# Every fourth weight group's low part made by an adding DMA

## The chip, the core and the metric

The kernel runs on one core of one Trainium2 chip. The metric is the device time of one execution in microseconds; lower is better. The core's engines are named as in the profile: PE multiplies matrices (PEld is its weight load), DVE is VectorE, ACT is ScalarE, POOL is GpSimd, and SP issues DMAs. 16 DMA engines serve the core.

## What is computed

One hybrid decoder layer on 256 tokens of width 2048: a gated FFN (width 5504) with a half residual, then a mixer whose input projection feeds a recurrent branch (RG-LRU) and a sparse attention branch (top 64 of the keys by an indexer), then a second FFN and a final norm.

```python
def reference(x, ...):
    x = x + 0.5 * swiglu(rms_norm(x, ffn1_norm), ffn1_w_gate, ffn1_w_up, ffn1_w_down)
    x = x + hybrid_mixer(rms_norm(x, mix_norm), w_in, ...)
    x = x + 0.5 * swiglu(rms_norm(x, ffn2_norm), ffn2_w_gate, ffn2_w_up, ffn2_w_down)
    return rms_norm(x, final_norm)

def swiglu(x, w_gate, w_up, w_down):
    return (silu(x @ w_gate) * (x @ w_up)) @ w_down

def hybrid_mixer(h, w_in, ...):
    rx, rgate, q, k, v, iq, ik, iw, g_rnn, g_attn = split(h @ w_in)
    y_rnn = rg_lru(conv(rx)) * gelu(rgate)
    y_attn = dsa_attention(q, k, v, iq, ik, iw, rel_bias)
    merged = sigmoid(g_rnn) * (y_rnn @ w_proj_rnn) + sigmoid(g_attn) * (y_attn @ w_proj_attn)
    return merged @ w_out
```

## The kernel before

All activations lie transposed, features on the 128 partitions and the 256 tokens along the row. Every matrix product is made in float32r with a split: a float32 value is a high part (rounded to float32r) and a low part (the value minus the high part). The activations are held as high and low side by side, 512 columns. For each 128x128 block of weights PE makes two matmuls: the high weights against all 512 columns (L111), and the low weights against the 256 high columns (L112).

The weights are read once, in order of use. A **group** is eight blocks, 128x1024 float32 or 512 KB, and is one row block of the array in HBM. `Stream` is the reader of one matrix. `load` (L79 and on) lets SP issue the DMA of one group into a tile `raw` from a pool of three. `pop` (L89 and on) hands out one block's pair; when the last group is used up it takes the next `raw` and makes two new tiles, `whi` and `wlo`, each from a pool of three, with `split` (L65 and on): ScalarE copies `raw` to `whi` (L68), and DVE subtracts `whi` from `raw` into `wlo` (L69). A tile of a pool is written anew when the tile of three groups earlier has been read for the last time, by PE for `whi` and `wlo`, by ScalarE and DVE for `raw`.

The products run in this order: FFN 1 (for each of 43 output blocks of the hidden width two groups of the gate matrix, then two of the up matrix; then for each of 16 output blocks 43 blocks of the down matrix, which is 5.4 groups); the small indexer columns; the streams iq, k, v, q, rx and rg (two groups an output block); the gate columns and the attention projection in turn (ga, pa), the same for the recurrent branch (gr, pr); out; FFN 2 as FFN 1. 806 groups pass through `wsp`, two of them by a path of its own for the indexer's columns.

Every engine works its instructions strictly in the order of its own queue. A scheduler at build time fixes that order, so an engine's row stands not quite where the Python line stands, but groups stay in order. After each product ScalarE copies one half of PSUM to SBUF (`tb`, L133), DVE adds the halves (`tt`, L135), and what follows belongs to the stage. GpSimd adds the squares for the norms (L178, L180), adds the attention biases to the mask (L507, L508) and issues a few loads, of which the 16 `xo` (L657), 128 KB each, are the largest. TensorE's clock is granted at one of two levels, 1.2 or 2.4 GHz; the profile gives it as a share of the higher one.

Of the kernel before, what the change touches and what calls it, by code (L numbers as in the profile page):

```python
# [11 lines left out]
F32 = mybir.dt.float32  # L12
F32R = mybir.dt.float32r
AF = mybir.ActivationFunctionType
ALU = mybir.AluOpType
# [3 lines left out]
P = 128  # L19
# [16 lines left out]
G = 8  # L36
# [7 lines left out]
def hybrid_layer(ctx: ExitStack, tc: tile.TileContext, a, out):  # L44
    nc = tc.nc
    V, A, T, GP = nc.vector, nc.scalar, nc.tensor, nc.gpsimd
# [18 lines left out]
    def split(hi, lo, src, scale=None):  # L65

        if scale is None:
            A.activation(hi, src, AF.Copy)  # L68
            V.tensor_tensor(lo, src, hi.bitcast(F32), op=ALU.subtract)  # L69
        else:  # L70
            A.activation(hi, src, AF.Copy, scale=scale)
            V.scalar_tensor_tensor(lo, src, scale, hi.bitcast(F32), op0=ALU.mult, op1=ALU.subtract)  # L72

    class Stream:


        def __init__(self, src):
            self.src, self.ahead, self.left, self.at = src, [], [], 0

        def load(self, parts=1):  # L80
            raw = wraw.tile([P, G * P], F32, name="raw")
# [7 lines left out]
        def pop(self):  # L89
            if not self.left:  # L90
                if not self.ahead:
                    self.load()
                raw = self.ahead.pop(0)
                hi = wsp.tile([P, G * P], F32R, name="whi")
                lo = wsp.tile([P, G * P], F32R, name="wlo")
                n, self.parts = G * P // self.parts, 1
                for i in range(0, G * P, n):
                    split(hi[:, i:i + n], lo[:, i:i + n], raw[:, i:i + n])
                self.left = [(hi[:, i * P:(i + 1) * P], lo[:, i * P:(i + 1) * P]) for i in range(G)]
            return self.left.pop(0)  # L100

# [287 lines left out]
    for k0 in range(0, KT, G):  # L389
        raw = wraw.tile([P, G * P], F32, name="raw")  # L390
        nc.sync.dma_start(raw[:, :G * 80], a["w_ikw"][:, k0 * 80:(k0 + G) * 80])
        hi = wsp.tile([P, G * P], F32R, name="whi")
        lo = wsp.tile([P, G * P], F32R, name="wlo")
# [365 lines left out]
```

## Time and profile before

| | |
|---|---|
| runs | 2343.24 and 2334.46 us, median 2338.85 |
| profiled execution | 2343.12 us, of which the span from the first to the last instruction is 2341.3 |
| PE busy | 2316.1 us, 99% |
| DVE busy | 1505.7 us, 64% |
| ACT busy | 1156.6 us, 49% |
| POOL busy | 95.0 us, 4% |
| weights and other bytes moved | 437.46 MB, 187 GB/s over the span |

A busy PE includes matmuls that overlap, so the share says that PE had work all the time, not that it ran at its peak. The rows below are of that one execution, with times in microseconds from the start of the span unless they are marked ns.

### The profile page before, as it was taken

What the parts mean: (1) busy time and instruction counts of PE and PEld (TensorE: products, weight loads), DVE (VectorE), ACT (ScalarE), POOL (GpSimd) and SP (SyncE); (2) the same over time, 40 slices, a digit from 0 to 9 for tenths busy, and PEclk for the clock granted to TensorE, in tenths of its full rate; (3) what the DMA queues carried; (4) which work ended last, traced back from release to release, by engine and by line L of the source; (5) the groups of instructions that cost most, each with busy time, mean ns of one, the idle gap of its engine ahead of it and who ended that gap; (6) DMA issues with size and microseconds to landing.
All of it is one profiled execution on the core that took longest, in us unless ns stands there. A gap on an engine that the chain in (4) does not pass through costs nothing.

```text
span 2341.3 us, 34677 instructions
## 1 busy us (share of the span) xinstructions
PE 2316.1 (99%) x13507; PEld 2024.9 (86%) x13507; DVE 1505.7 (64%) x2238; ACT 1156.6 (49%) x1689; POOL 95.0 (4%) x137
## 2 busy tenths in 40 slices
PE   8999999999999999999999999999999999999998
PEld 6888888888888888998888888888888888888887
DVE  6766666655555687778855566676666666664444
ACT  6444444444444455677644444455544444444443
POOL 0000000000000011001000000021000000000000
PEclk9999999999999999999999999999999999999999
DMA  6555555556565544454565655666665665566664
GB/s 219 184 190 192 190 189 189 189 192 199 199 199 193 201 162 144 152 182 161 175 191 186 188 185 186 193 209 200 189 189 189 189 190 190 189 191 192 191 189 144
DMA packets 128548, 437.46 MB, mean 187 GB/s; under 512 B 14416, under 2 KB 22976, under 8 KB 128384
## 3 DMA queue, kind: packets, MB, share of 16 engines
q1 hardware_dynamic: 127296, 432.84, 56.7%
q8 instruction: 105, 1.72, 0.3%
q0 software_dynamic: 912, 2.33, 0.3%
q14 instruction: 59, 0.48, 0.1%
q10 hardware_dynamic: 176, 0.09, 0.0%
HBM read 430.92 MB, written 4.22 MB: 186 GB/s over the span
## 4 chain that ended last, share of the span: by engine, by line
PE 94%; DVE 3%; DMA 1%; ACT 1%; issue 1%; SPq 0%; POOL 0%; DVEq 0%; ACTq 0%
PE mm L111 58%; PE mm L112 29%; PE mm L126 2%; PE mm L125 2%; PE mm L127 2%; DVE wlo L69 1%; DMA raw<-in_w_rg 1%; ACT whi L68 0%; DMA raw<-in_wu 0%; PE aux L435 0%; PE aux L575 0%; PE aux L576 0%; DVE hst L622 0%; PE aux L505 0%; DMA raw<-in_wg 0%
## 5 line engine op out<-in xcount | busy, mean ns | idle before, releaser
L69 DVE TENSOR_TENSOR wlo<-raw,whi 128x1024 fp32r<-128x1024 f32 (+2 forms) x807 | 987.0, 1223 | 729.8 <-ACT whi L68 727.4
L68 ACT ACTIVATE whi<-raw 128x1024 fp32r<-128x1024 f32 (+2 forms) x807 | 853.6, 1058 | 1116.9 <-PE mm L111 560.0
L111 PE MATMUL mm<-x1hl,whi 128*128 128x512 f32 x1376 | 482.5, 397 | 8.1 <-DVE x1hl L72 7.4
L111 PE MATMUL mm<-x3hl,whi 128*128 128x512 f32 x1376 | 477.3, 394 | 0.0
L111 PE MATMUL mm<-h,whi 128*128 128x512 f32 x1333 | 462.2, 394 | 0.0
L111 PE MATMUL mm<-x2hl,whi 128*128 128x512 f32 x1280 | 457.1, 400 | 0.0
L112 PE MATMUL mm<-x1hl,wlo 128*128 128x256 f32 x1376 | 384.2, 279 | 1.8 <-DVE wlo L69 1.8
L112 PE MATMUL mm<-x3hl,wlo 128*128 128x256 f32 x1376 | 381.8, 278 | 0.0
L112 PE MATMUL mm<-h,wlo 128*128 128x256 f32 x1333 | 369.7, 277 | 0.0
L112 PE MATMUL mm<-x2hl,wlo 128*128 128x256 f32 x1280 | 360.1, 281 | 3.6 <-DVE wlo L69 3.3
L111 PEld LDWEIGHTS mm<-x1hl,whi 128*128 128x128 f32 x1376 | 260.3, 189 | 69.8 <-ACT whi L68 7.6
L111 PEld LDWEIGHTS mm<-x3hl,whi 128*128 128x128 f32 x1376 | 258.5, 188 | 59.2
L111 PEld LDWEIGHTS mm<-h,whi 128*128 128x128 f32 x1333 | 250.5, 188 | 57.6
L111 PEld LDWEIGHTS mm<-x2hl,whi 128*128 128x128 f32 x1280 | 240.8, 188 | 57.5 <-issue 0.7
L112 PEld LDWEIGHTS mm<-x1hl,wlo 128*128 128x128 f32 x1376 | 260.2, 189 | 3.2 <-DVE wlo L69 3.1
L112 PEld LDWEIGHTS mm<-x3hl,wlo 128*128 128x128 f32 x1376 | 258.4, 188 | 0.0
L112 PEld LDWEIGHTS mm<-h,wlo 128*128 128x128 f32 x1333 | 250.2, 188 | 0.0
L112 PEld LDWEIGHTS mm<-x2hl,wlo 128*128 128x128 f32 x1280 | 241.8, 189 | 6.7 <-DVE wlo L69 5.8
L135 DVE TENSOR_TENSOR tt<-mm,tb 128x256 f32<-128x256 f32 x285 | 118.8, 417 | 1.8 <-ACT tb L133 1.8
L133 ACT ACTIVATE tb<-mm 128x256 f32<-128x256 f32 x285 | 104.2, 366 | 2.0 <-DVE zero L151 2.0
L142 DVE TENSOR_TENSOR tz<-tt,rstd 128x256 f32<-128x256 f32 x224 | 94.8, 423 | 6.9
L111 PE MATMUL mm<-yat,whi 128*128 128x512 f32 x256 | 91.2, 399 | 0.0
(192 smaller groups left out, 1987.6 us busy)
## 6 DMA issues: line engine op xcount, KB each, us to landing
raw<-in_wu SPq DMA_DIRECT2D x172, 512.0 KB, 3.6
raw<-in_wd SPq DMA_DIRECT2D x172, 512.0 KB, 4.1
raw<-in_wg SPq DMA_DIRECT2D x171, 512.0 KB, 3.6
raw<-in_w_q SPq DMA_DIRECT2D x32, 512.0 KB, 3.4
raw<-in_w_rx SPq DMA_DIRECT2D x32, 512.0 KB, 3.4
raw<-in_w_rg SPq DMA_DIRECT2D x32, 512.0 KB, 3.5
raw<-in_w_ga SPq DMA_DIRECT2D x32, 512.0 KB, 3.6
raw<-in_w_pa SPq DMA_DIRECT2D x32, 512.0 KB, 3.6
```

Source lines behind the costliest of these rows:

```text
L68: A.activation(hi, src, AF.Copy)
L69: V.tensor_tensor(lo, src, hi.bitcast(F32), op=ALU.subtract)
L111: T.matmul(ps, hi, x, start=(k == 0), stop=False)
L112: T.matmul(ps[:, S:], lo, x[:, :S], start=False, stop=(k == kts - 1))
L125: T.matmul(ps[:, :S], hi, x[:, :S], start=(k == 0), stop=False)
L126: T.matmul(ps[:, :S], hi, x[:, S:], start=False, stop=False)
L127: T.matmul(ps[:, :S], lo, x[:, :S], start=False, stop=(k == kts - 1))
L133: A.activation(b[:M], ps[:M, S:], AF.Copy)
L135: V.tensor_tensor(t[:M], ps[:M, :S], b[:M], op=ALU.add)
L142: V.tensor_tensor(o, t, r, op=ALU.mult)
```

## The change

Each `Stream` counts its groups. Three of four are made as before. For every fourth, ScalarE writes the high part (L100 in the changed kernel) and then the negated high part into the low tile (L101), and GpSimd issues a DMA that reads the same group from HBM a second time and adds it to what lies in the low tile (L102). SP's load of the group into `raw` stays, since the high part is made from it. Lines after L105 stand seven lines further down in the changed kernel (L111 is L118, L112 is L119, L133 is L140).

```diff
         def __init__(self, src):
-            self.src, self.ahead, self.left, self.at = src, [], [], 0
+            self.src, self.ahead, self.left, self.at, self.popped = src, [], [], 0, 0
@@ def pop(self):
                 n, self.parts = G * P // self.parts, 1
-                for i in range(0, G * P, n):
-                    split(hi[:, i:i + n], lo[:, i:i + n], raw[:, i:i + n])
+                self.popped += 1
+                if self.popped % 4 == 0:
+
+                    A.activation(hi, raw, AF.Copy)
+                    A.activation(lo, hi.bitcast(F32), AF.Copy, scale=-1.0)
+                    GP.dma_start(lo, self.src[self.popped - 1], accum_op=ALU.add)
+                else:
+                    for i in range(0, G * P, n):
+                        split(hi[:, i:i + n], lo[:, i:i + n], raw[:, i:i + n])
```

Where it lies in the queues. The next two fences are ScalarE's queue in FFN 1 around the fourth output block's gate and up groups. `h` is the split of a hidden block, `sg` its silu, `tb` the copy out of PSUM; what stands in brackets is what the instruction waits for (PE, DVE, Activation for ScalarE itself, DMAHW for SP's and DMASW for GpSimd's DMAs). Before:

```order
L68 ACTIVATE whi_527<-raw_525 128x1024 [waits DMAHW6_49,PE_49,Activation_49]
L238 ACTIVATE sg_382<-tz_380 128x256 [waits DVE_49]
L133 ACTIVATE tb_384<-mm_303 128x256 [waits Activation_49]
L68 ACTIVATE whi_550<-raw_548 128x1024 [waits DMAHW7_49,PE_49,Activation_49]
L68 ACTIVATE h_115<-h_390 128x256 [waits DVE_49]
L133 ACTIVATE tb_484<-mm_394 128x256
L68 ACTIVATE whi_572<-raw_570 128x1024 [waits DMAHW0_49,PE_49,Activation_49]
L238 ACTIVATE sg_490<-tz_488 128x256 [waits DVE_49,Activation_49]
L133 ACTIVATE tb_492<-mm_439 128x256 [waits Activation_49]
L68 ACTIVATE whi_613<-raw_611 128x1024 [waits DMAHW1_49,PE_49,Activation_49]
L68 ACTIVATE h_115<-h_498 128x256 [waits DVE_49]
```

After:

```order
L140 ACTIVATE tb_386<-mm_304 128x256
L100 ACTIVATE whi_529<-raw_527 128x1024 [waits DMAHW6_49,PE_49,Activation_49]
L101 ACTIVATE wlo_530<-whi_529 128x1024 [waits DMASW5_49,PE_49,Activation_49]
L68 ACTIVATE h_115<-h_392 128x256 [waits DVE_49]
L140 ACTIVATE tb_486<-mm_396 128x256
L68 ACTIVATE whi_553<-raw_551 128x1024 [waits DMAHW7_49,PE_49]
L245 ACTIVATE sg_492<-tz_490 128x256 [waits DVE_49]
L140 ACTIVATE tb_494<-mm_441 128x256 [waits PE_49]
L100 ACTIVATE whi_575<-raw_573 128x1024 [waits DMAHW0_49,PE_49]
L68 ACTIVATE h_115<-h_500 128x256 [waits DVE_49]
L101 ACTIVATE wlo_576<-whi_575 128x1024 [waits DMASW4_49,PE_49,Activation_49]
```

The groups `whi_529` and `whi_575` (`whi_527` and `whi_572` before) are adding ones: behind each high part stands the negated copy into `wlo`, the second time with a split of `h` between the two. Between them lies one ordinary group, `whi_553`. The order of the others is kept.

GpSimd's queue from the loads of the start to the first sums of squares, before:

```order
L297 DMA ident_103<-in_ident 128x128
L299 DMA cw_105<-in_conv_w 128x64
L301 DMA CM_107<-in_causal 128x256
L303 DMA rb_109<-in_rel_bias 32x16
L178 COPY sqsum_4996<-sq_4994 128x256 [waits DVE_49,PE_49,Activation_49]
L180 ISA
L180 TENSOR_TENSOR sqsum_4996<-sqsum_4996,sq_5122 128x256 [waits Activation_49,Pool_49]
```

After, from the same load on:

```order
L310 DMA rb_109<-in_rel_bias 32x16
L102 DMA wlo_274<-in_wg1 128x1024 [waits DVE_49,PE_49,Activation_49]
L102 DMA wlo_330<-in_wu1 128x1024 [waits DVE_49,Activation_49]
L102 DMA wlo_530<-in_wg1 128x1024 [waits DMASW5_49,DVE_49,Activation_49]
L102 DMA wlo_576<-in_wu1 128x1024 [waits DMASW4_49,DVE_49,Activation_49]
L102 DMA wlo_787<-in_wg1 128x1024 [waits DMASW0_49,DMASW7_49,DVE_49,Activation_49]
L102 DMA wlo_833<-in_wu1 128x1024 [waits DMASW1_49,DVE_49,Activation_49]
```

The adding loads now stand where GpSimd had nothing to do: all of the gate and up matrices' come ahead of the first `sqsum`, in the order of the groups, each behind a wait for ScalarE's copy. In the down stage they alternate with the `sqsum` additions.

PE's queue at the start of such a group, before (an ordinary group at the same place):

```order
L112 MATMUL mm_502<-x1hl_111,wlo_506 128x256
L111 MATMUL mm_502<-x1hl_111,whi_527 128x512 [waits Activation_49]
L112 MATMUL mm_502<-x1hl_111,wlo_528 128x256 [waits DVE_49]
L111 MATMUL mm_502<-x1hl_111,whi_527 128x512
L112 MATMUL mm_502<-x1hl_111,wlo_528 128x256
```

After:

```order
L119 MATMUL mm_504<-x1hl_111,wlo_508 128x256
L118 MATMUL mm_504<-x1hl_111,whi_529 128x512 [waits Activation_49]
L119 MATMUL mm_504<-x1hl_111,wlo_530 128x256 [waits DMASW6_49]
L118 MATMUL mm_504<-x1hl_111,whi_529 128x512
L119 MATMUL mm_504<-x1hl_111,wlo_530 128x256
```

The order of the matmuls is the same. The first matmul with `wlo_530` waits for GpSimd's DMA, where the one with `wlo_528` waited for DVE, and it stands second in its group.

## Rows read from the trace of the kernel before

**Rows 1.** The page, busy us (share) xinstructions, and granted clock over 40 slices

```profile
PE 2316.1 (99%) x13507; PEld 2024.9 (86%) x13507; DVE 1505.7 (64%) x2238; ACT 1156.6 (49%) x1689; POOL 95.0 (4%) x137
...
PEclk9999999999999999999999999999999999999999
```

**Rows 2.** The page, chain of work that ended last, by engine and line

```profile
PE 94%; DVE 3%; DMA 1%; ACT 1%; issue 1%; SPq 0%; POOL 0%; DVEq 0%; ACTq 0%
PE mm L111 58%; PE mm L112 29%; PE mm L126 2%; PE mm L125 2%; PE mm L127 2%; DVE wlo L69 1%; DMA raw<-in_w_rg 1%; ACT whi L68 0%; DMA raw<-in_wu 0%; PE aux L435 0%; PE aux L575 0%; PE aux L576 0%; DVE hst L622 0%; PE aux L505 0%; DMA raw<-in_wg 0%
```

**Rows 3.** Waits: engine, line, waited for: us in total, times, longest us

```profile
PEld mm L112 <- DVE wlo L69: 8.9, 11, 1.4
...
PE mm L112 <- DVE wlo L69: 5.2, 7, 1.1
```

**Rows 4.** Timeline in FFN 1: start us, us, instruction [idle before, releaser]

```profile
401.38 1.06 ACT L68 ACTIVATE whi<-raw 128x1024 fp32r<-128x1024 f32 x1 [1.41 <-PE mm L111]
...
402.35 0.36 ACT L133 ACTIVATE tb<-mm 128x256 f32<-128x256 f32 x1
...
402.47 1.23 DVE L69 TENSOR_TENSOR wlo<-raw,whi 128x1024 fp32r<-128x1024 f32 x1 [1.21 <-ACT whi L68]
...
404.15 1.06 ACT L68 ACTIVATE whi<-raw 128x1024 fp32r<-128x1024 f32 x1 [1.44 <-PE mm L111]
```

**Rows 5.** The page, costliest groups: count, busy us, mean ns, idle before

```profile
L69 DVE TENSOR_TENSOR wlo<-raw,whi 128x1024 fp32r<-128x1024 f32 (+2 forms) x807 | 987.0, 1223 | 729.8 <-ACT whi L68 727.4
L68 ACT ACTIVATE whi<-raw 128x1024 fp32r<-128x1024 f32 (+2 forms) x807 | 853.6, 1058 | 1116.9 <-PE mm L111 560.0
```

**Rows 6.** SP's loads by stream: issue ns min/median/max, first to last start us

```profile
L84 SPq DMA_DIRECT2D raw<-in_w_q x32: 327/328/328, 824.2 to 933.5; - x32
L84 SPq DMA_DIRECT2D raw<-in_w_rx x32: 327/328/328, 936.0 to 1044.4; - x32
L84 SPq DMA_DIRECT2D raw<-in_w_rg x32: 327/328/332, 1048.1 to 1145.7; - x32
...
L84 SPq DMA_DIRECT2D raw<-in_w_iq x16: 327/328/542, 728.2 to 771.7; - x16
```

**Rows 7.** DMA: queue's packets, MB, share; loads' count, KB, us to landing

```profile
q1 hardware_dynamic: 127296, 432.84, 56.7%
...
raw<-in_wu SPq DMA_DIRECT2D x172, 512.0 KB, 3.6
...
xo<-x1d POOLq DMA_DIRECT2D x16, 128.0 KB, 3.4
...
wa<-in_rg_w_a SPq DMA_DIRECT2D x16, 64.0 KB, 2.6
...
DMA to landing us min/median/max: 2.4/3.4/5.1
```

**Rows 8.** Windows at the start: busy by engine, granted clock, DMA share, GB/s

```profile
12.00:16.00 4.00, 4.00 (x22) 3.19 (x20) 4.00 (x9) 3.97 (x9) 0.00 (x0) 1.00 1.02 400
```

**Rows 9.** Timeline of PE at the start

```profile
25.88 0.51 PE L111 MATMUL mm<-x1hl,whi 128*128 128x512 f32 x1
26.83 0.50 PE L111 MATMUL mm<-x1hl,whi 128*128 128x512 f32 x1 [0.44 <-ACT whi L68]
28.40 0.39 PE L112 MATMUL mm<-x1hl,wlo 128*128 128x256 f32 x1 [1.06 <-DVE wlo L69]
```

**Rows 10.** Windows of one us behind it, columns as in group 8

```profile
29.00:30.00 1.00, 1.00 (x7) 0.89 (x6) 1.00 (x2) 0.00 (x0) 0.00 (x0) 0.75 0.41 131
30.00:31.00 1.00, 1.00 (x4) 0.80 (x4) 1.00 (x2) 0.00 (x0) 0.00 (x0) 0.50 0.88 344
31.00:32.00 1.00, 1.00 (x5) 0.90 (x4) 1.00 (x2) 0.00 (x0) 0.00 (x0) 0.50 0.48 131
32.00:33.00 1.00, 1.00 (x5) 0.83 (x5) 0.75 (x3) 0.00 (x0) 0.00 (x0) 0.54 0.92 344
```

## The prediction

> **What bounds the kernel now.** I read the page's busy table first, then the chain that ended last, the waits, and a timeline of one steady stretch. In the busy table the reader is to see one engine that never rests: PE is busy 99% of the span, DVE 64%, ACT 49%, at a granted clock in the top tenth throughout [rows 1]. The chain says the same by line: 94% of it is PE, 87% the two matmul lines L111 and L112, and DVE has 3%, a third of that the low parts (L69) [rows 2]. The waits say how little PE now waits for the low parts: 5.2 us in 7 places, and its weight load 8.9 us in 11 [rows 3]. So DVE's work on the low parts is hidden, and taking work off DVE can give back at most a part of those 14 us.
>
> What hides it is the lead that the pool of three split buffers gives. ScalarE starts the high part of a group when PE lets go of the buffer of three groups earlier, so two whole groups of matmuls lie between that moment and PE's first need of the new group. ScalarE's starts are 2.77 us apart (401.38, 404.15) [rows 4], so the lead is 2 x 2.77 = **5.54 us**. Of it the kernel uses 2.32 us: the low part that starts at 402.47 takes 1.23 us and is ready 2.32 us after 401.38 [rows 4]. 3.2 us are to spare. The question is whether the new way to the low part fits into 5.54 us.
>
> **The change part by part.** *Count.* Each of the six FFN matrices has 86 groups (172 for two of a kind, [rows 7] and the loops), so 21 adding loads each, 126 in all; the iq, k and v streams have 4, 2 and 2, and q, rx, rg, ga, pa, gr, pr and out 8 each. That is 198.
>
> *What goes.* 198 subtractions on DVE at 1.22 us [rows 5], 242 us of DVE's 1506. DVE is not on the path; a quarter of the 14 us of waits, some 3.5 us, is the most it gives. I take nothing.
>
> *What ScalarE gets.* 198 more passes over 128x1024. The high part's pass takes 1.06 us [rows 5], the same shape and engine, so 210 us, and ScalarE goes from 1157 to 1367 us, 58% of the span. That is hidden as work, but in an adding group it stands in the chain: 1.06 for the high part, then the negated copy, 1.06. By the order of the changed kernel 124 of the 198 have another short activation in between; at the 0.36 us of the tb copy in the timeline [rows 4], or slightly more, that is 0.25 us on the mean. So 1.06 + 0.25 + 1.06 = **2.37 us** until GpSimd may issue, and 5.54 - 2.37 = 3.17 us are left for the adding load.
>
> *What the adding load takes.* The trace has no accumulating transfer. From below: SP's plain load of the same 512 KB lands 3.6 us after its issue [rows 7]. Nearest by queue: the 128 KB loads that GpSimd issues (xo) land after 2.4 to 5.1 us, median 3.4 [rows 7]. Already that median, for a quarter of the bytes, is above 3.17. For size I take SP's own rows: 64 KB lands in 2.6, 512 KB in 3.6, 1.0 us for 448 KB, so 384 KB more are 0.9 us, and a plain 512 KB load from GpSimd is 4.3 us. The add must also fetch what lies in the low tile. I take that as a second pass of 512 KB through the 16 engines: they moved 400 GB/s when fully busy [rows 8], 1.31 us for 512 KB. The raw loads hold the engines 57% of the time [rows 7], so I stretch it to 1.31 x 1.57 = 2.06 us. The adding load is then 3.4 + 0.9 + 2.0 = **6.3 us**, between 4.3 (no second pass) and 8.4 (two more passes).
>
> The rate of an add in a DMA engine is where I have only a page for a check. The Trainium skill, Collectives: The Full Stack, section "The bandwidth ceiling: the fold count and why AG ≠ RS ≠ AR", says that a reducing transfer runs at half the rate of a copying one because it reads two sources; no run here shows it. By it the second pass is right, and by a plain-copy rate the sum would be the low bound below.
>
> *What the path loses.* The chain of an adding group is 2.37 + 6.3 = 8.67 us. PE stops behind the first hi matmul of the group, because the lo matmul next in its queue waits for the load; every later matmul is queued behind it. Where the next adding group is four groups on, its buffer comes free after the stop, so each stop counts in full. Where gate and up (and ga/pa, gr/pr) alternate, adding groups come as pairs two groups apart, in every second product: the buffer of the second was freed before the first stopped, so its lead is 5.54 plus that stop, 8.67, and it just fits. Pairs: 42 in the FFNs, 16 in the gated projections. Singles: 42 in the down matrices, 8 in out, 32 in iq, k, v, q, rx and rg. At the FFN's pace 42 + 16 + 42 + 8 = 108 places stop for 8.67 - 5.54 = 3.13 us: 338 us. In the others a group takes longer, by the first and last of their loads [rows 6]: q 109.3 / 31 = 3.53 us, rx 3.50, rg 3.15, iq 2.90 (taken for k and v too). Their leads are 7.06, 7.0, 6.3 and 5.8, the stops 1.61, 1.67, 2.37 and 2.87, eight of each: 13 + 13 + 19 + 23 = 68 us. Together **406 us**.
>
> *What a stop does to the clock.* The trace has one such place. Between 25.88 and 28.40 PE ran two matmuls of 0.5 us and otherwise waited for ScalarE and DVE [rows 9]; the granted clock, 1.00 before, was 0.75, 0.50, 0.50 and 0.54 in the four microseconds from 29 [rows 10], the lower level of 1.2 GHz, for 1.7 us of lost work. The new stops are of that length, but most of the time around them is busy, so I charge it at half of the 140 places: **119 us**. Bounds: none, and all, 238.
>
> *The queues.* GpSimd was 4% busy with little queued; an adding load stands behind its sums of squares (down stages) and attention adds (q stage), whose inputs ScalarE or DVE make earlier in order, so I add nothing. The load's bytes are 198 x 0.52 = 104 MB on 437. An engine pass of 512 KB costs 0.567 x 2341.3 / (432.84 / 0.524) = 1.6 us [rows 7]; two passes 198 times are 634 us on 1327, which would be 84% of the old span: busy, not full. SP's raw loads are released earlier in an adding group (by ScalarE, not DVE), a small help to a queue that isn't late.
>
> *Sum.* The profiled execution took 2343.12 us, 0.2% above the median of the runs shown, 2338.85. 2343 + 406 + 119 = 2868; I say **2870 us**.
>
> **The rivals.**
> 1. *The load lands in time, and nothing changes* (the other side). If it lands as SP's does, in 3.6 us, the chain is 5.97, PE stops 0.43 us at 108 places, and the time is 2343 + 46 + 1 = 2390. Below 3.17 us there are no stops and the time is 2340, with the 3.5 us of DVE waits back. It decides at 3.6 us. For it: xo's fastest is 2.4. Against it: xo's median is 3.4 with a quarter of the bytes. The Trainium skill, DMA: Bandwidth & Descriptors, section "Anatomy of one DMA — SWDGE (gpsimd) path", gives 2.0 us plus bytes over 436 GB/s; my estimate from that is 3.2 us for 512 KB, and the time would be this rival's. Its fit is of plain loads; by xo's 3.4 for 128 KB, where it would give 2.3, the trace is slower. 0.07.
> 2. *One pass only.* 4.3 us: the chain is 6.67; 1.13 x 108 + 8 x (0.37 + 0.87) = 132, no falls of the clock: 2475. 0.13.
> 3. *The add is slow in the engines.* At three more passes the load takes 3.4 + 0.9 + 6.2 = 10.5 us, the chain 12.9: 7.3 x 108 + 8 x (5.8 + 5.9 + 6.6 + 7.1) = 991, the clock at all 140 places 238, and the second of a pair, whose load overlaps the first, up to 2 us at 58 places, 116: 3690. For it: no row bounds the rate of an add. 0.15, two thirds of it above 3350.
> 4. *The forecast*, two passes, with the clock anywhere between none and all: 0.65.
>
> **How the numbers follow.** Low end: rival 2, 2475, taken as 2470. High end: 8.4 us, chain 10.8: 5.2 x 108 + 8 x (3.7 + 3.8 + 4.5 + 5.0) = 698, clock 238, pairs some 70: 3350. Below lie rival 1 and a part of rival 2, above two thirds of rival 3: together 2 in 10. A measurement of this kernel tells about 2% from no change, here 47 us. Faster by that much: 0.02, since only the 14 us of waits and the DVE pieces of the chain could be won. Within it: 0.05, rival 1. Slower: 0.93.
>
> **What would show it.** Right: PE's wait for the low parts goes from some 14 us to several hundred, and the releaser is the adding load, in about 140 places and not 198; the adding load's row says some 6 us from issue to landing; pairs show one long and one short stop; DVE's busy time falls by 240 us, ScalarE's rises by 210, and neither moves the time; the granted clock shows 0.5 after some stops. Wrong: a landing under 3.6 us; stops at 198 places, which would mean that the pairs don't overlap; DMA busy near its full share, which would make rate and not landing the cause; or ScalarE's negated copy waiting behind something other than its high part.

## The result and the profile after

The changed kernel takes **3066.12 us** (median of two runs, 3062.14 and 3070.10) against 2338.85 before: a ratio of **1.311, 95% interval 1.298 to 1.324**. The forecast was 2870 with a range of 2470 to 3350, slower at 0.93. The direction, the mechanism and the range held; the loss, 727 us between the two profiled spans, is larger than the 525 that were worked out.

The page of the changed kernel: busy us with shares by engine; the granted clock in 40 slices; the DMA queues with packets, MB and their share of 16 engines; the chain by engine. In the rows below, L118 and L119 are the two matmul lines and L102 is the adding load.

```profile
PE 2569.9 (84%) x13507; PEld 2201.5 (72%) x13507; DVE 1275.8 (42%) x2040; ACT 1357.5 (44%) x1887; POOL 257.0 (8%) x335
...
PEclk8999999999988999998999989988999999988888
...
q1 hardware_dynamic: 127296, 432.84, 42.5%
q0 software_dynamic: 29424, 106.15, 20.4%
...
PE 38%; DMA 31%; issue 22%; ACT 6%; DVE 3%; POOL 0%; POOLq 0%; SPq 0%; DVEq 0%; ACTq 0%
```

PE is no longer always busy: 84% instead of 99% [rows 1]. The chain that was PE for 94% [rows 2] now runs through DMA for 31%; its 22% of issue is time for which the profile names no releaser. DVE lost 230 us of work and ScalarE gained 201, and neither amount moved the end: PE had waited 5.2 us for DVE's low parts [rows 3], and the first experiment shows it for ScalarE. PE's busy time itself rose by 254 us, with the same 13507 matmuls.

Waits of PE for the low parts, with total us, times and longest us; then the adding loads with their KB and median us from issue to landing, and the extremes over all 198:

```profile
PE mm L119 <- DMA wlo<-in_wd: 155.3, 41, 5.0
PE mm L119 <- DMA wlo<-in_wg: 143.4, 42, 4.5
...
PE mm L119 <- DMA wlo<-in_wu: 1.7, 1, 1.7
...
wlo<-in_wg POOLq DMA_DIRECT2D x42, 512.0 KB, 6.9
wlo<-in_wu POOLq DMA_DIRECT2D x42, 512.0 KB, 7.1
wlo<-in_wd POOLq DMA_DIRECT2D x42, 512.0 KB, 7.2
...
DMA to landing us min/median/max: 5.5/7.1/10.7
```

Where 5.2 us of PE's waits were for the low parts [rows 3], all rows of this kind for adding loads now add up to 475.6 us in 138 places. The gate's 42 and the down's 42 (one by another line) stop PE; of the up's 42, the second of each pair, one does. So the loss of 727 us is 476 of waiting and 254 of longer matmuls.

One stop, from a timeline in FFN 1 (start, duration, what ran, and in brackets the idle time before it with its releaser), and the windows of one us behind it (busy by PE, PEld, DVE, ACT and POOL, granted clock, DMA share, GB/s):

```profile
494.84 1.06 ACT L100 ACTIVATE whi<-raw 128x1024 fp32r<-128x1024 f32 x1 [1.49 <-issue]
495.81 0.40 ACT L245 ACTIVATE sg<-tz 128x256 f32<-128x256 f32 x1
495.93 4.36 SPq L84 DMA_DIRECT2D raw<-in_wg  x2
496.11 1.04 ACT L101 ACTIVATE wlo<-whi 128x1024 fp32r<-128x1024 f32 x1
497.45 0.85 POOL L102 DMA_DIRECT2D wlo<-in_wg  x1 [20.86 <-ACT wlo L101]
...
503.61 0.38 PE L119 MATMUL mm<-x1hl,wlo 128*128 128x256 f32 x1 [2.62 <-DMA wlo<-in_wg]
```

```profile
503.00:504.00 1.00, 0.39 (x2) 0.39 (x3) 0.00 (x0) 0.00 (x0) 0.85 (x1) 0.97 0.98 377
504.00:505.00 1.00, 1.00 (x5) 0.80 (x4) 0.00 (x0) 0.00 (x0) 0.00 (x0) 0.50 0.99 381
505.00:506.00 1.00, 1.00 (x4) 0.87 (x4) 0.00 (x0) 0.00 (x0) 0.00 (x0) 0.50 1.22 324
506.00:507.00 1.00, 1.00 (x5) 0.83 (x4) 0.00 (x0) 0.00 (x0) 0.00 (x0) 0.50 0.96 184
507.00:508.00 1.00, 1.00 (x7) 0.86 (x7) 0.00 (x0) 0.09 (x1) 0.00 (x0) 0.82 1.01 201
```

ScalarE starts at 494.84, GpSimd issues 2.61 us later, the load lands a little before 503.61, and PE has idled for 2.62 us although the chain was given two groups. Between the two, at 495.93, SP has issued its next raw load, just as ScalarE's first pass ended. Behind the stop the clock is at 0.50 for a little over three us: PE works through the group it waited for at half speed.

### The profile page after: what moved, and what is told of

It reads as the page before. It is cut to its first block, busy times and chain, and to the rows that moved or that the text cites. A ratio compares the mean times of both kernels' runs of the same rounds, so it can differ in the third digit from the quotient of the medians.

```text
span 3068.3 us, 35229 instructions
## 1 busy us (share of the span) xinstructions
PE 2569.9 (84%) x13507; PEld 2201.5 (72%) x13507; DVE 1275.8 (42%) x2040; ACT 1357.5 (44%) x1887; POOL 257.0 (8%) x335
## 3 DMA queue, kind: packets, MB, share of 16 engines
q0 software_dynamic: 29424, 106.15, 20.4%
## 4 chain that ended last, share of the span: by engine, by line
PE 38%; DMA 31%; issue 22%; ACT 6%; DVE 3%; POOL 0%; POOLq 0%; SPq 0%; DVEq 0%; ACTq 0%
PE mm L118 22%; PE mm L119 13%; DMA wlo<-in_wd 10%; DMA wlo<-in_wg 9%; DVE wlo L69 2%; ACT whi L68 2%; DMA wlo<-in_w_gr 2%; ACT wlo L101 2%; DMA wlo<-in_w_rg 2%; DMA wlo<-in_w_ga 2%; DMA wlo<-in_w_out 2%; ACT whi L100 2%; DMA wlo<-in_w_q 2%; DMA wlo<-in_w_rx 1%; DMA wlo<-in_w_iq 1%
## 5 line engine op out<-in xcount | busy, mean ns | idle before, releaser
L69 DVE TENSOR_TENSOR wlo<-raw,whi 128x1024 fp32r<-128x1024 f32 (+1 forms) x609 | 745.9, 1225 | 1410.7 <-ACT whi L68 1386.2
L68 ACT ACTIVATE whi<-raw 128x1024 fp32r<-128x1024 f32 (+1 forms) x609 | 643.7, 1057 | 1347.3 <-PE mm L118 1065.5
L119 PE MATMUL mm<-h,wlo 128*128 128x256 f32 x1333 | 407.1, 305 | 155.3 <-DMA wlo<-in_wd 155.3
L118 PE MATMUL mm<-h,whi 128*128 128x512 f32 x1333 | 524.3, 430 | 0.0
L118 PE MATMUL mm<-x1hl,whi 128*128 128x512 f32 x1376 | 513.0, 416 | 7.5 <-DVE x1hl L72 7.0
L118 PE MATMUL mm<-x3hl,whi 128*128 128x512 f32 x1376 | 511.9, 416 | 0.0
L118 PE MATMUL mm<-x2hl,whi 128*128 128x512 f32 x1280 | 506.3, 431 | 0.0
L119 PE MATMUL mm<-x2hl,wlo 128*128 128x256 f32 x1280 | 390.4, 305 | 130.4 <-DMA wlo<-in_w_gr 32.2
L119 PE MATMUL mm<-x3hl,wlo 128*128 128x256 f32 x1376 | 398.5, 294 | 75.4 <-DMA wlo<-in_wg 75.3
L119 PE MATMUL mm<-x1hl,wlo 128*128 128x256 f32 x1376 | 398.4, 294 | 71.8 <-DMA wlo<-in_wg 68.1
L119 PEld LDWEIGHTS mm<-h,wlo 128*128 128x128 f32 x1333 | 282.4, 212 | 168.3 <-DMA wlo<-in_wd 168.3
L119 PEld LDWEIGHTS mm<-x2hl,wlo 128*128 128x128 f32 x1280 | 269.5, 211 | 146.2 <-DMA wlo<-in_w_gr 35.7
L119 PEld LDWEIGHTS mm<-x3hl,wlo 128*128 128x128 f32 x1376 | 278.5, 202 | 88.0 <-DMA wlo<-in_wg 84.1
L119 PEld LDWEIGHTS mm<-x1hl,wlo 128*128 128x128 f32 x1376 | 277.4, 202 | 85.0 <-DMA wlo<-in_wg 76.8
L100 ACT ACTIVATE whi<-raw 128x1024 fp32r<-128x1024 f32 x198 | 209.8, 1060 | 270.9 <-PE mm L118 176.7
L118 PEld LDWEIGHTS mm<-h,whi 128*128 128x128 f32 x1333 | 280.0, 210 | 67.4
L118 PEld LDWEIGHTS mm<-x1hl,whi 128*128 128x128 f32 x1376 | 273.1, 200 | 71.9 <-ACT whi L68 7.1
L118 PEld LDWEIGHTS mm<-x3hl,whi 128*128 128x128 f32 x1376 | 273.4, 201 | 62.5
L118 PEld LDWEIGHTS mm<-x2hl,whi 128*128 128x128 f32 x1280 | 266.9, 209 | 63.0 <-issue 0.7
L101 ACT ACTIVATE wlo<-whi 128x1024 fp32r<-128x1024 f32 x198 | 207.7, 1049 | 2.3
L102 POOL DMA_DIRECT2D wlo<-in_wg x42 | 36.0, 857 | 892.1 <-ACT wlo L101 820.3
```

The lines of the kernel that those rows point to most:

```text
L100: A.activation(hi, raw, AF.Copy)
L101: A.activation(lo, hi.bitcast(F32), AF.Copy, scale=-1.0)
L102: GP.dma_start(lo, self.src[self.popped - 1], accum_op=ALU.add)
L118: T.matmul(ps, hi, x, start=(k == 0), stop=False)
L119: T.matmul(ps[:, S:], lo, x[:, :S], start=False, stop=(k == kts - 1))
```

## The experiments

Each kernel is the changed one with one thing altered, except the control with four buffers, which is made from the kernel before, and the last, which joins two alterations. Time to landing is counted from the start of GpSimd's issue, so it contains the issue. The two terms to test are the stop (landing against lead) and the clock; the disputed size is the landing. `ADD` stands for the line `GP.dma_start(lo, self.src[self.popped - 1], accum_op=ALU.add)`.

### ScalarE's passes without the load

```diff
-ADD
+V.tensor_tensor(lo, raw, lo.bitcast(F32), op=ALU.add)
```

> The adding groups keep ScalarE's two passes (high part, negated high part), but DVE adds the weights to the low tile instead of GpSimd's DMA. Theory (PE stops because the adding load lands after the 5.54 us of lead): the chain is 1.06 + 0.25 + 1.06 + 1.23 = 3.6 us, inside the lead, so no stops, the clock stays, and the time is that of before, 2340 within 0.5%. Rival (ScalarE's 198 extra passes, 208 us in the profile, and what they push back in its queue carry a good part of the loss): 2450 to 2550, with PE waiting for ScalarE or DVE.

2367.56 us, ratio 1.012 (1.009 to 1.015). The waits of PE for the low parts by DVE, and PE's busy time:

```profile
PE mm L119 <- DVE wlo L69: 3.9, 5, 1.1
...
PE 2341.1 (99%) x13507; PEld 2034.6 (86%) x13507; DVE 1505.3 (64%) x2238; ACT 1353.0 (57%) x1887; POOL 87.1 (4%) x137
```

So 198 more passes on ScalarE make PE wait for next to nothing (0.6 us, once, for DVE's add), and the rival falls. The time is not quite that of before, though: 25 us are left, outside the half per cent expected, and all of them are in PE's busy time (2341.1 against 2316.1 in [rows 1]), not in waits. What that is stands in the last section. As work, ScalarE's passes have at most these 25 us in the loss of 727. As latency they count: the second pass, 1.05 us, stands in the chain of every adding load, ahead of its issue.

### A plain load at the same place

```diff
-ADD
+GP.dma_start(lo, self.src[self.popped - 1])
```

> The same load at the same place, issued by GpSimd behind ScalarE's two passes, but as a plain copy over the low tile; the low part is then the whole weight and the output is not the layer's. Theory (the second pass of the add through the DMA engines makes the landing long): landing 4.3 to 5 us instead of 7.1, stops of 1.1 to 1.9 us, few falls of the clock, 2480 to 2620 us. Rival (what GpSimd needs to make the descriptors, and its queue among the others, makes it long, and the add itself is nearly free): landing still 6.5 to 7.1 us, and 2980 to 3070 us.

2622.40 us, ratio 1.121 (1.117 to 1.126), 2 us above the expected range. The loads and the queue's share:

```profile
q0 software_dynamic: 29424, 106.15, 12.9%
...
wlo<-in_wg POOLq DMA_DIRECT2D x42, 512.0 KB, 4.8
wlo<-in_wu POOLq DMA_DIRECT2D x42, 512.0 KB, 5.0
wlo<-in_wd POOLq DMA_DIRECT2D x42, 512.0 KB, 4.9
...
DMA to landing us min/median/max: 3.7/4.9/7.1
```

The plain load lands in 4.9 us where the adding one needs 7.1, so the add costs 2.2 us of landing at this place, and the rival (GpSimd's issue is all of it) falls: the issue takes 0.53 us instead of 0.85, which is 0.3 of the 2.2. The engines' time says the same: the queue's 12.9% of 2618 us, over 198 loads, is 1.7 us each; the adding load's 20.4% of 3068 us is 3.2 us. The same bytes written cost 1.9 times the engine time. The Trainium skill, Collectives: The Full Stack, section "The bandwidth ceiling: the fold count and why AG ≠ RS ≠ AR", says of ring collectives that a reduction has half the rate of a copy, for its two source reads; this pair of runs agrees with the factor and doesn't show the reason. But even the plain load is too late: with 4.9 us PE still waits 202.5 us, in 152 places.

### The add from the raw tile

```diff
-ADD
+GP.dma_start(lo, raw, accum_op=ALU.add)
```

> The adding load takes the weights from the raw tile in SBUF, which SP has loaded already, instead of reading them from HBM again: 104 MB less from HBM, the same number of bytes through the DMA engines. Theory (two passes through the engines and GpSimd's fixed part, not HBM, set the landing): landing 6 to 7.1 us and 2900 to 3070 us. Rival (the second read from HBM, beside SP's loads of 190 GB/s, is what is slow): landing 4.5 to 5.2 us and 2500 to 2650 us. In both the raw tile is held until the add has landed, so SP's load of three groups later starts some 7 us later than now, which may add up to 2 us a place.

2722.90 us, ratio 1.164 (1.159 to 1.169), between the two figures, with the landing of the rival:

```profile
q0 software_dynamic: 29424, 106.15, 20.6%
...
wlo<-raw POOLq DMA_DIRECT2D x198, 512.0 KB, 4.7
...
PE mm L119 <- DMA wlo<-raw: 268.5, 177, 4.9
```

4.7 us instead of 7.1, although the engine time of a load is still 20.6% of 2717 us over 198, 2.8 us. So the two passes alone do not make the 7.1, as the theory had it. Two things differ here: the source, and that SP's next load cannot start while the raw tile is held. This run cannot tell them apart; the next one does. Taken one by one in the trace, the 4.7 is that of 140 loads (median 4.6); the 58 seconds of the pairs land in 6.7, though they read nothing from HBM. PE waits in 185 places now (8 of them by another line), the seconds of the pairs too.

### The add from HBM with the raw tile held

```diff
 ADD
+held_raw = tmp.tile([P, 1], F32, name="held_raw")
+GP.tensor_tensor(held_raw, raw[:, :1], lo[:, :1].bitcast(F32), op=ALU.add)
```

> The adding load reads HBM as in the changed kernel, but a one-column addition on GpSimd reads the raw tile and the low tile behind it, so SP's load into that raw tile starts only when the add has landed, as it did in the run whose add came from the raw tile. Theory (the add's landing of 7.1 us is made long by SP's load that starts at the same time, as the 4.7 us of the add from the raw tile, which ran without it, suggests): landing 4.9 to 5.5 us and 2700 to 2850 us, with late raw loads as part of what is left. Rival (the second read from HBM is what takes the time): landing 6.5 to 7.1 us and 3000 to 3200 us.

2859.43 us, ratio 1.223 (1.217 to 1.229).

```profile
wlo<-in_wg POOLq DMA_DIRECT2D x42, 512.0 KB, 5.5
wlo<-in_wu POOLq DMA_DIRECT2D x42, 512.0 KB, 7.5
wlo<-in_wd POOLq DMA_DIRECT2D x42, 512.0 KB, 5.5
...
DMA to landing us min/median/max: 5.2/5.6/9.1
```

The add from HBM lands in 5.6 us at the median instead of 7.1. The edit alters two things: when SP's load may start, and that GpSimd waits for each landing, which delays the issue of the up's loads, the seconds of pairs, by 0.4 us at the median. The gate's and the down's loads are issued as soon behind ScalarE as before, and they fall from 6.9 and 7.2 to 5.5, so there the delay of SP's load is what differs. So of the 2.4 us between 7.1 and 4.7, some 1.5 come from SP's load, which the changed kernel starts as soon as ScalarE has read the raw tile (behind the stop shown above, where the up's add and SP's loads are under way, the engines are at 0.96 and more of their time). The other 0.9 is what is left for the read of HBM; the seconds of pairs differ by about as much, 7.5 here (the up's) against 6.7. The up's loads still meet SP's: in the trace SP's loads of 7.2 us in sum are under way beside one of them, 3.4 beside one of the gate's. Neither expectation had the size quite (4.9 to 5.5, and 2850 at most); the direction is that of the theory. Without SP's load the add would still be late by the lead.

### Singles instead of pairs

```diff
-        def __init__(self, src):
+        def __init__(self, src, add=True):
...
-                if self.popped % 4 == 0:
+                if self.add and self.popped % 4 == 0:
...
+# add=False for wg1, wg2, w_ga and w_gr
```

> Only the second adding group of each pair is kept: the gate matrices of both FFNs, ga and gr are split as before, so 140 adding loads instead of 198, each now alone. Theory (a single stops PE for its full lateness, and the second of a pair is hidden by the stop of the first): as many stops as now, 140, of the same length, and nearly the same time, 3000 to 3070 us. Rival (each adding load costs its share, by engine time, bytes or GpSimd's issue): 727 x 140 / 198 = 514 us over before, 2855 us.

3025.57 us, ratio 1.293 (1.288 to 1.299), with 58 adding loads less.

```profile
PE mm L119 <- DMA wlo<-in_wd: 148.2, 41, 5.0
...
PE mm L119 <- DMA wlo<-in_wu: 130.2, 42, 4.4
...
DMA to landing us min/median/max: 5.4/6.8/9.2
```

The up's 42 loads, which cost 1.7 us behind the gate's, cost 130 when they stand alone, and PE waits in 137 places, 449 us, against 138 and 476. The price is by stop, not by load: 29% fewer loads bring 41 us of 727, and 27 of these are waits. The rival's 2855 is far off.

### One more buffer

```diff
-T1 = 12
+T1 = 5
...
-    wsp = ctx.enter_context(tc.tile_pool(name="wsp", bufs=3))
+    wsp = ctx.enter_context(tc.tile_pool(name="wsp", bufs=4))
```

> The changed kernel with four split buffers for the high and low tiles instead of three; the small tiles' pool shrinks from 12 to 5 to make room. Theory (lead): the lead grows by one group, 2.77 us, to 8.3 us; the chain is 5.54 + some 3.6 = 9.1 to 9.5 us, so a stop is 0.8 to 1.2 us, the clock stays, and the time is 2450 to 2520 us. Rival (the DMA engines' rate or GpSimd's issue is the limit, or the smaller pool makes waits of its own): above 2800 us.

2526.74 us, ratio 1.081 (1.074 to 1.088), 7 us above the expected range. The waits and the landing:

```profile
PE mm L119 <- DMA wlo<-in_wg: 39.3, 37, 4.8
...
PE mm L119 <- DMA wlo<-in_wd: 29.7, 25, 1.8
...
DMA to landing us min/median/max: 5.3/7.1/10.6
```

The loads land as late as before, 7.1 us, the engines are as busy with them, and 540 of 727 us are gone: the waits fall from 476 to 137 us and PE's busy time from 2569.9 to 2369.8. That is the lead, and it rules out the DMA engines' rate as the bound of the changed kernel. The gate's stop, 143.4 / 42 = 3.4 us before, is now 39.3 / 37 = 1.1. It fell by 2.3, somewhat less than the 2.77 us of a group.

The control has the same two lines in the kernel before:

> The kernel before, with four split buffers and the small pool of 5 instead of 12: the control of the run with four buffers. Theory (the kernel before never lacked lead, and the smaller pool costs nothing): within 1% of before, so what the four-buffer version of the change still lost is its adding loads. Rival (the smaller pool costs most of the 190 us which that version was above before): 2450 to 2530 us.

2352.61 us, ratio 1.009 (1.006 to 1.011), within the 1% expected. The smaller pool is not what lead4 lost.

### Work in the stops

```diff
+                self.fill = 14 if self.first and self.popped % 4 == 0 else 0
...
             T.matmul(ps, hi, x, start=(k == 0), stop=False)
+            if w.fill:
+                idle = aux.tile([P, 2 * S], F32, name="aux")
+                for i in range(w.fill):
+                    T.matmul(idle, hi, x, start=True, stop=True)
+                w.fill = 0
...
+# first=False for wu1, wu2, w_pa and w_pr
```

> The changed kernel, with 14 idle matmuls of 128x512 (some 3.0 us at the high clock) into a PSUM tile that nobody reads, put between the first high and the first low matmul of each adding group that stops PE (not in the second of a pair). They run while PE would wait some 3.4 us. Theory (about a third of the loss, 254 us of longer PE busy time, is the clock that falls after each stop): the stops stay as long, the clock stays near 1, and the time falls by 200 to 250 us to 2820 to 2870 us, though more work is done. Rival (the longer matmuls have another cause, such as the DMA traffic on SBUF): no gain, 3050 to 3150 us.

2909.48 us, ratio 1.245 (1.238 to 1.251): 157 us less than the changed kernel with 1834 matmuls more. The gain is below the 200 expected. The page's first line, the granted clock, and the idle matmuls (L123) in a timeline and in a window of 400 us of FFN 1:

```profile
PE 2786.7 (96%) x15341; PEld 2381.3 (82%) x15341; DVE 1276.1 (44%) x2040; ACT 1353.8 (47%) x1887; POOL 253.8 (9%) x335
...
PEclk9999999999999999999999999999999999999999
...
494.18 3.38 PE L123 MATMUL aux<-x1hl,whi 128*128 128x512 f32 x14
...
100.00:500.00 400.00, 50.51 (x210) 39.43 (x210) 1.00 0.72 195
```

The mean granted clock is 0.993 instead of 0.915. 14 idle matmuls take 50.51 / 15 = 3.37 us, 441 us at 131 places, so PE's own work is 2786.7 - 441 = 2346 us, 30 above before and not 254; the run where DVE adds, without a load, was 25 above. The idle matmuls and the 98.5 us of waits that are left come to 540 us, 64 more than the waits that they replace, since not every stop was that long; 254 - 30 - 64 = 160 us, the gain. So some 220 of the 254 us, 254 - 30, were the clock.

### Halves, and both together

```diff
-A.activation(lo, hi.bitcast(F32), AF.Copy, scale=-1.0)
-ADD
+for h in (slice(0, G * P // 2), slice(G * P // 2, G * P)):
+    A.activation(lo[:, h], hi[:, h].bitcast(F32), AF.Copy, scale=-1.0)
+    GP.dma_start(lo[:, h], self.src[self.popped - 1][:, h], accum_op=ALU.add)
```

> The negated copy and the adding load of a group are made in two halves of 512 columns, so the first four blocks can be used when the first half has landed. Theory (landing has a fixed part of some 3 us and a part by size; PE needs only the first half at first): the first half is issued 0.5 us earlier and lands in 5 to 5.5 us, a stop falls by 1.5 to 2.5 us, few falls of the clock, 2600 to 2800 us. Rival (landing is fixed, not by size, and two loads queue behind each other): 3000 to 3150 us.

2792.75 us, ratio 1.195 (1.187 to 1.202), at the slow end of what was expected. All adding loads, of 256 KB now:

```profile
DMA to landing us min/median/max: 4.0/6.3/9.8
```

The waits fall to 307 us, PE's busy time to 2453.7. Halves help. That half the bytes still take 6.3 us at the median does not price the size, since the two halves of a group are in flight together: the trace has the first halves at 5.8, where 5 to 5.5 were expected, and the second at 6.8.

> Four split buffers and the adding load in two halves, both steps that shortened the stops by themselves. Theory (a stop is what is left of the landing over the lead): the halves take 1.3 us off a stop, four buffers 2.77 us, and 3.4 to 3.8 us were lost; little is left and the time is 2350 to 2420 us, near before but not below it, since PE then waits for nothing that the change could take away. Rival (two loads on GpSimd and more DMA work leave a loss of their own): above 2450 us.

2413.86 us, ratio 1.032 (1.029 to 1.036). PE waits for adding loads 35.4 us in 40 places. The other half of the 67 us between the spans is PE's busy time, 2350.4 against 2316.1. This is the best version of the change, still 3% above the kernel before; no version beat that, since it left PE next to nothing to wait for.

## Why the prediction was right, and where its sizes were off

**The bound and the lead.** Right. PE was the bound, and the way to the low part had 5.54 us. In the stop shown PE idles from 500.99 (503.61 less 2.62), behind the group's first high matmul of 0.40 us: the lead from ScalarE's start at 494.84 to that matmul was 5.75 us, near the 5.54. One buffer more took 340 us of waits away with the landing unchanged; one pass more on ScalarE took none.

**ScalarE's chain, 2.37 us.** Near: 2.61 in the stop shown, with `sg` between the two passes and, which the sum did not have, 0.3 us until GpSimd's issue. The passes on ScalarE added 201 us of work (210 expected) and DVE lost 230 (242 expected), and neither moved the end as work.

**The landing, 6.3 us.** Too small: 7.1. Both of its parts were a little low. The plain load, put at 4.3, is 4.9: xo's 3.4 and SP's slope were not enough. The second pass, put at 2.06, is 2.2. The engine time was right: 634 us were reckoned for the 198 loads, and 20.4% of 3068.3 is 626. The landing was near for a reason that was only half of it: the add takes 1.9 times the engine time, but with SP's load held back it lands in 5.6 us, and some 1.5 of the 7.1 are SP's load beside it. The factor of 1.57 for the raw loads' mean share stood for that. But a raw load is released by the same ScalarE pass that leads to the add, 1.5 us ahead of its issue in the stop shown, and in the trace each of the 198 adding loads has SP's loads beside it. The prediction saw this earlier release and called it a small help; it was part of the cost. Unstretched, the sum's terms give 3.4 + 0.9 + 1.31 = 5.6, as measured with SP's load held back; the stretch added 0.75 for SP's loads where some 1.5 were measured. The agreement at 5.6 may be luck in part, as xo's 3.4 was itself measured beside SP's loads.

**The stops, 406 us.** 476. In the gate a stop is 3.4 us instead of 3.13, in the down matrices 155.3 / 41 = 3.8. With the landing 0.8 us and ScalarE's chain 0.2 us longer more would have been expected, some 1.0 x 138 = 138 us on the 406 against 70 measured. The sum had counted a stop from the group's start, but PE still runs the group's first high matmul, 0.40 us here, before it idles: 0.40 x 138 = 55 us of the difference.

**Pairs.** Right, and the sharpest point of the sum: 138 places where 140 were counted, though there are 198 loads; one of the up's 42 loads stopped PE, and alone all 42 did.

**The clock, 119 us.** The term most off: some 220 us of the 254 in PE's busy time, about the upper bound that was named, 238. The charge at half of the places was wrong: 220 / 138 = 1.6 us a place, near the 1.7 that was read for one. The row it came from, a fall behind a stretch of 2.5 us with two matmuls [rows 9, 10], was the right one, and the stops, of 3.4 us, were longer than that stretch; nothing in the rows spoke for half. The changed kernel's trace says much the same: the granted clock fell to 0.50 behind 120 of the 138 stops, and PE was busy for 468 us at that level, half of which, some 234 us, is lost. Had all 140 been charged, and the landing put at 7.1, the stops would have come to 3.93 x 108 + 8 x (2.4 + 2.5 + 3.2 + 3.7) = 519 and the sum to 2343 + 519 + 238 = 3100, near the 3066 measured.

**The rivals.** *Lands in time* (it decided at 3.6 us): the fastest of all 198 adding loads took 5.5, and even the plain one took 4.9 at the median, 3.7 at the fastest. The fit of the Trainium skill, DMA: Bandwidth & Descriptors, section "Anatomy of one DMA — SWDGE (gpsimd) path", from which 3.2 us was worked out, is below both medians; here the measurements decide, with SP's loads on the same engines. *One pass only* (2475): the plain load, which is that case, took 2622: 202.5 us of waits where 132 were worked out, with 0.6 us more of landing, and 76 us more in PE's busy time (2392.1 against 2316.1) where none was. Some 25 of these 76 came without a stop too, in the run where DVE adds; the clock fell behind 14 of the 152 stops, and PE was busy for 57 us at 0.50, half of them lost; the rest is open. *The add slow in the engines* (3690): 1.9 times, not four. DMA's two queues took 63% of the longer span, and four buffers took 340 of 476 us of the stops away with the same bytes to move.

## What to carry to other kernels

A producer for a fully busy engine is judged by its latency against the lead that the buffers give, not by the work that it takes off another engine: here 230 us came off an engine that nobody waited for, and the way round it was some 9 us long where two groups gave 5.5. Count the stops by where the next buffer comes free, since a second late load in the shadow of a first costs nothing, and charge each stop of some three us with the clock behind it, 1.6 us on the mean here. If a transfer has to stay in such a path, give it one more buffer first (540 of 727 us), then look at what other load the same step releases onto the same DMA engines.

## What was not expected of the hardware

An adding load of 512 KB from SBUF, with 1.7 times the engine time of a plain one (2.8 us against 1.7), landed in 4.7 us at the median when SP's load was held back, no later than the plain load from HBM beside SP's (4.9). Engine time and landing are not the same thing.

TensorE's pace also differs by some 2% between stages at the full clock, with nothing to wait for. The first fence is from the kernel before, the second from the run where DVE adds; columns are count, duration ns min/median/max, first and last start us:

```profile
L111 PE MATMUL mm<-x3hl,whi x1376: 391/393/477, 1610.8 to 2088.4; 128*128 128x512 f32 x197
...
L111 PE MATMUL mm<-yat,whi x256: 395/398/404, 1165.6 to 1340.5; 128*128 128x512 f32 x128
```

```profile
L118 PE MATMUL mm<-x3hl,whi x1376: 392/398/477, 1621.7 to 2108.3; 128*128 128x512 f32 x197
```

The same products of FFN 2 took 393 ns a matmul before and 398 in that run, and this over whole stages; the first attention projection's (`yat`) took 398 before. From the start of one matmul of 512 columns to that of the next, in the traces, the mean is 347 ns before in FFN 1, FFN 2 and out and 353 in that run, and some 353 for `yat` in both. Over the 4341 blocks of those three stages that is some 27 us; PE's busy time rose by 25, which is all that that run was slower. The control with four buffers has FFN 2 at 398 too, and 11.5 us more PE time; the changed kernel with four buffers has means between the two. What sets the pace stays open; the runs show only that no wait of PE's goes with it.
